# Where a causal convolution's running sums lie, which engine takes which taps, and where its group norms stand

## The chip, the core and the metric

The kernel runs on one core of one Trainium2 chip. Four engines compute: TensorE (PE in the rows; PEld is its weight load), VectorE (DVE), ScalarE (ACT) and GpSimd (POOL). SyncE (SP) issues most of the loads. SBUF is the large on-chip memory, PSUM the small one of eight banks into which TensorE writes; a bank holds 512 float32 values in each of 128 partitions. The metric is the device time of one execution in microseconds, the median over runs.

## What is computed

Two decoder layers for 256 tokens of width 1024, all in float32. The change touches the mixer of the first layer, whose two head groups share one input projection and one output projection:

```
u = h @ w_in                                   # 2560 columns
u_conv, u_sb = split(u, [1024])
val, gate = split(u_conv, 2)                   # 512 channels each
y = val * sigmoid(gate)
y = causal_depthwise_conv(y, conv_w) + conv_b  # 31 taps per channel
mean and variance of y over each 64 channels   # 8 groups
a_out = silu((y - mean) * rsqrt(var + 1e-5) * norm_g + norm_b)
b_out = stick_breaking_attention(q, k, v from u_sb)   # 8 heads of 64
mix = concat([a_out, b_out]) @ w_out
```

Behind it come a mixture of experts, the second layer's mixer, a second mixture of experts and a last norm.

## The kernel before

Activations lie transposed: channels in the partitions, the 256 tokens along the row. The 512 convolution channels are four tiles `yp[:, k]` of 128x286 (30 zeros ahead of the tokens), so tap `j` of tile `k` is the slice `yp[:, k, j:j + T]` times one weight per partition. There are 4 x 31 = 124 such taps.

**The projections** (class `Projections`, line 434 for transposed outputs, 429 for natural ones) run five times over 1024 input channels: gate, val, q, k, v. Each has eight steps; a step takes one granule of weights, 128x512, split into a high and a low part (`split`, lines 60 and 61: ScalarE copies the high part, VectorE subtracts), and twelve matmuls (six in the natural form) of TensorE. Granules are split two steps ahead. In the projections of q, k and v a callback `step` behind every step issues some taps through `conv(n, m)`: `n` from the generator `taps`, `m` from `other_taps`.

**The taps.** `taps` is VectorE's share, 59 of them: 16 of tile 2, 12 of tile 1 and all of tile 0, each a scalar_tensor_tensor (line 570) that reads the running sum and writes it back, in SBUF (`yc`). `other_taps` is the share of the other two engines, 65: all of tile 3, the last 15 of tile 2, 19 of tile 1 in a sum of its own (`more`); ScalarE multiplies into a small buffer (line 584, three buffers), GpSimd adds (line 585). At its end VectorE adds `more` to tile 1 (line 587).

**The heads.** Four passes `cc`, of two heads each. A pass has the sums over later keys on TensorE (`sums`, tile `zc`), VectorE's subtraction (`weights`, lines 666 and 667), ScalarE's exponential (line 668), the attention product (`attend`, line 680) and its split (`attended`, lines 685 and 686). Between these stand taps, `fill(n)` (steps of the conditioning matmuls, line 195, which need no result of the mixer) and, in the third pass, the first weights of the output product.

**The group norms.** `group_norm(h)` for two tiles at a time: a mean by a matmul with a block matrix (`gm`, line 691), VectorE's subtraction (692), ScalarE's square, a second matmul (`gv`, 697), reciprocal root on VectorE and ScalarE (699 to 701), VectorE's product (703). It is a generator; the code advances `gn[0]` (tiles 0 and 1) and `gn[1]` (tiles 2 and 3) by hand.

**The output product** (class `Output`, line 464) takes the heads' half first, in eight steps, then the convolution's half.

The order on every engine is the order of the code (a manual schedule). PSUM banks for short-lived tiles come from `bank`: two of the tag `ps`, one of the tag `pq`, in turn. Weights stream through a ring of 16 buffers of 1 MB; a load is issued when the buffer's last reader is done.

Of the kernel before, what the change touches and what calls it, by code (L numbers as in the profile page):

```python
# [15 lines left out]
T = 256  # L16
# [13 lines left out]
def trunk(ctx: ExitStack, tc: tile.TileContext, x, c, ada_w, ada_b, norm_mix, norm_ffn,  # L30
# [14 lines left out]
    turn = [0]  # L45

    def bank(name, two=False):
        tag, bufs = ("ps", 2) if two or turn[0] % 3 < 2 else ("pq", 1)
        turn[0] += not two
        return psum.tile([128, 512], F32, tag=tag, name=name, bufs=bufs)  # L50
# [459 lines left out]
    def even_mixer(pool, n01, late):  # L510
# [49 lines left out]

        def taps():

            sums = [[(2, j) for j in range(16)] + [(1, j) for j in range(12)], [(0, j) for j in range(31)]]
            while any(sums):
                sums.sort(key=len)
                k, j = sums[1].pop(0)
                if j == 0:
                    V.tensor_scalar(yc[:, k], yp[:, k, 0:T], epar[:, k, 0:1], epar[:, k, 31:32], op0=OP.mult, op1=OP.add)
                else:
                    V.scalar_tensor_tensor(yc[:, k], yp[:, k, j:j + T], epar[:, k, j:j + 1], yc[:, k],  # L570
                                           op0=OP.mult, op1=OP.add)
                yield

        def other_taps():
            more = pool.tile([128, T], F32, name="more")
            for k, js, y in ((3, range(31), yc[:, 3]), (2, range(16, 31), yc[:, 2]), (1, range(12, 31), more)):
                for j in js:
                    if k == 3 and j == 0:
                        G.tensor_scalar(y, yp[:, k, 0:T], epar[:, k, 0:1], epar[:, k, 31:32], op0=OP.mult, op1=OP.add)
                    elif k == 1 and j == 12:  # L580
# [5 lines left out]
                    yield  # L586
            V.tensor_tensor(yc[:, 1], yc[:, 1], more, op=OP.add)
# [13 lines left out]
        with tc.tile_pool(name="pj0", bufs=4, space=bass.MemoryType.PSUM) as banks:  # L601
# [10 lines left out]
            project(1, val)  # L612
            project(2, lambda h, b: S.activation(qT[:, 2 * h:2 * h + 2], b, AF.Copy, scale=0.125),
                    step=lambda k: conv(1 + k % 2, 1 + k % 2))
            project(3, lambda h, b: S.activation(kT[:, 2 * h:2 * h + 2], b, AF.Copy),
                    step=lambda k: conv(1 + k % 2, 1 + k % 2))
            vn = pool.tile([128, 2, 512], F32, tag="sv", name="vn")
            project(4, lambda t, b: S.activation(vn[:, t], b, AF.Copy), True, step=lambda k: conv(1 + k % 2, 1 + k % 2))
# [92 lines left out]
        conv(2, 4)  # L711
        minus(0)
        softplus(0)
        conv(2, 0)
# [3 lines left out]
        conv(2, 2)  # L718
        for cc in range(4):
# [26 lines left out]
        next(gn[1])  # L746
        next(steps)
        next(gn[1])
        next(gn[0])
# [940 lines left out]
```

## Time and profile before

| | |
|---|---|
| median of 3 runs | 781.63 us (779.17 to 783.79) |
| the profiled execution | 781.72 us, its span 780.0 us |
| TensorE busy | 720.2 us, 92% of the span |
| VectorE busy | 315.1 us, 40% |
| ScalarE busy | 235.0 us, 30% |
| GpSimd busy | 120.8 us, 15% |
| read from HBM | 280.59 MB, 361 GB/s over the span |

The shares are means over stages with different limits. The mixer of the first layer runs from about 33 to 180 us; its last three projections from 57.7 to 102 us, the heads from 104 to 145 us, the output product to about 180 us. The first experts start near 200 us.

### The profile page before, as it was taken

What the parts mean: (1) busy time and instruction counts of PE and PEld (TensorE: products, weight loads), DVE (VectorE), ACT (ScalarE), POOL (GpSimd) and SP (SyncE); (2) the same over time, 40 slices, a digit from 0 to 9 for tenths busy, and PEclk for the clock granted to TensorE, in tenths of its full rate; (3) what the DMA queues carried; (4) which work ended last, traced back from release to release, by engine and by line L of the source; (5) the groups of instructions that cost most, each with busy time, mean ns of one, the idle gap of its engine ahead of it and who ended that gap; (6) DMA issues with size and microseconds to landing.
All of it is one profiled execution on the core that took longest, in us unless ns stands there. A gap on an engine that the chain in (4) does not pass through costs nothing. (4 is left out here: it accounts for less than half of the span.)

```text
span 780.0 us, 10577 instructions
## 1 busy us (share of the span) xinstructions
PE 720.2 (92%) x4121; PEld 395.7 (51%) x4121; DVE 315.1 (40%) x567; ACT 235.0 (30%) x441; POOL 120.8 (15%) x168
## 2 busy tenths in 40 slices
PE   6898788898999999999888899999999999999995
PEld 4398643476434434443234577678534335444333
DVE  3459979475204113122114846454512214113214
ACT  3457667454102102111112535453401101001012
POOL 1357658022000000000003600010300000000000
PEclk9999999999999999999999999999899999999999
DMA  8999759953999999999999998497699999999994
GB/s 356 384 373 420 313 196 409 360 204 147 353 411 409 409 410 408 409 409 409 409 408 397 394 411 341 165 394 301 258 379 411 409 408 409 409 410 409 409 407 159
DMA packets 74712, 282.45 MB, mean 362 GB/s; under 512 B 5194, under 2 KB 6438, under 8 KB 69530
## 3 DMA queue, kind: packets, MB, share of 16 engines
q1 hardware_dynamic: 73122, 278.68, 91.1%
q0 software_dynamic: 1344, 2.64, 0.9%
q8 instruction: 34, 0.56, 0.3%
q10 hardware_dynamic: 184, 0.34, 0.1%
q14 instruction: 28, 0.23, 0.1%
HBM read 280.59 MB, written 1.05 MB: 361 GB/s over the span
## 5 line engine op out<-in xcount | busy, mean ns | idle before, releaser
L1272 PE MATMUL g<-w,xg 128*64 128x512 f32 x512 | 114.8, 597 | 1.9 <-DMA w<-in_moe_w_gate_dram 1.8
L1272 PE MATMUL u<-w,xg 128*64 128x512 f32 x496 | 111.3, 595 | 3.9 <-DMA w<-in_moe_w_up_dram 3.0
L1305 PE MATMUL dn<-w,at 128*64 128x512 f32 x448 | 100.2, 596 | 3.0 <-DMA w<-in_moe_w_down_dram 1.8
L1284 DVE TENSOR_TENSOR act<-sg,u 128x512 f32<-128x512 f32 (+1 forms) x18 | 11.1, 628 | 155.8 <-PE u L1272 155.8
L1272 PEld LDWEIGHTS u<-w,xg 128*64 128x64 f32 x496 | 34.7, 137 | 74.4 <-issue 62.7
L1272 PEld LDWEIGHTS g<-w,xg 128*64 128x64 f32 x512 | 35.0, 137 | 68.3 <-issue 60.5
L434 PE MATMUL pj<-hT,g 128*128 128x256 f32 x480 | 61.3, 285 | 6.1 <-DVE g L61 4.8
L61 DVE TENSOR_TENSOR g<-wi,g 128x512 fp32r<-128x512 f32 x72 | 57.0, 801 | 23.6 <-ACT g L60 23.4
L1305 PEld LDWEIGHTS dn<-w,at 128*64 128x64 f32 x448 | 31.4, 137 | 64.0 <-issue 55.4
L434 PEld LDWEIGHTS pj<-hT,g 128*128 128x128 f32 x480 | 57.7, 188 | 10.1 <-DVE g L61 6.9
L464 PE MATMUL po<-cat,g 128*128 128x256 f32 x372 | 52.9, 296 | 3.9 <-ACT gsr L1026 1.7
L60 ACT ACTIVATE g<-wi 128x512 fp32r<-128x512 f32 x72 | 44.4, 626 | 38.2 <-PE pj L434 20.7
L429 PE MATMUL pj<-g,hT 128*128 128x512 f32 x192 | 50.3, 412 | 6.0 <-ACT hT L355 3.1
L464 PEld LDWEIGHTS po<-cat,g 128*128 128x128 f32 x372 | 48.1, 201 | 9.3 <-issue 2.7
L195 PE MATMUL ada<-ad,cond 128*32 128x512 f32 x384 | 49.6, 626 | 3.0 <-DMA ad<-in_ada_w_dram 3.0
L429 PEld LDWEIGHTS pj<-g,hT 128*128 128x128 f32 x192 | 35.6, 193 | 20.1 <-DVE g L61 4.2
L570 DVE SCALAR_TENSOR_TENSOR yc<-yp,epar,yc 128x256 f32<-128x256 f32 x56 | 41.5, 756 | 2.2 <-POOL yc L585 1.7
L585 POOL TENSOR_TENSOR yc<-yc,cv 128x256 f32<-128x256 f32 x45 | 39.2, 872 | 19.7 <-ACT cv L584 12.0
L1295 DVE COPY at<-at 128x512 f32<-128x512 f32 x14 | 9.7, 692 | 67.3 <-PE at L1294 67.3
L1337 ACT ACTIVATE ys<-y 128x512 fp32r<-128x512 f32 x28 | 16.9, 625 | 64.2 <-DVE y L1327 59.3
L1280 ACT ACTIVATE sg<-g 128x512 f32<-128x512 f32 x14 | 8.4, 597 | 89.3 <-PE g L1272 89.3
L1331 ACT ACTIVATE y<-dn,cw 128x512 f32<-128x512 f32 x7 | 4.8, 687 | 100.5 <-PE dn L1305 100.5
(381 smaller groups left out, 869.8 us busy)
## 6 DMA issues: line engine op xcount, KB each, us to landing
w<-in_moe_w_gate_dram SPq DMA_DIRECT2D x64, 1024.0 KB, 15.5
w<-in_moe_w_up_dram SPq DMA_DIRECT2D x62, 1024.0 KB, 18.5
w<-in_moe_w_down_dram SPq DMA_DIRECT2D x61, 1024.0 KB, 18.1
ad<-in_ada_w_dram SPq DMA_DIRECT2D x48, 1024.0 KB, 9.0
wi<-in_w_in_even_dram SPq DMA_DIRECT2D x20, 512.0 KB, 12.2
wi<-in_w_in_odd_dram SPq DMA_DIRECT2D x14, 512.0 KB, 12.5
wo<-in_w_out_even_dram SPq DMA_DIRECT2D x4, 1024.0 KB
wo<-in_w_out_odd_dram SPq DMA_DIRECT2D x4, 1024.0 KB, 18.1
```

The costliest lines, as they stand in the source:

```text
L60: S.activation(g[0], w, AF.Copy)
L61: (eng or V).tensor_tensor(g[1], w, g[0].bitcast(F32), op=OP.subtract)
L195: PE.matmul(acc[32 * j:32 * j + 32, :], lhsT=cond[:, k, :], rhs=w[:, k - (i if n == 2 else 2 * i), c0:c0 + 512], start=i == 0, stop=i == 4 ...
L429: PE.matmul(bs[t], lhsT=self.h[j][:, k, t * 128:(t + 1) * 128], rhs=g[i], start=k == 0 and p == 0, stop=k == 7 and p == 2)
L434: PE.matmul(bs[c // 2][:, (c % 2) * T:(c % 2 + 1) * T], lhsT=g[i][:, c * 128:(c + 1) * 128], rhs=self.h[j][:, k, :], start=k == 0 and c % ...
L464: PE.matmul(self.acc[kd // 2][:, (kd % 2) * T:(kd % 2 + 1) * T], lhsT=block(g[wi], kd % 4), rhs=cats[ci][:, k, :], start=start and kd % 2 ...
L570: V.scalar_tensor_tensor(yc[:, k], yp[:, k, j:j + T], epar[:, k, j:j + 1], yc[:, k], op0=OP.mult, op1=OP.add)
L585: G.tensor_tensor(y, y, p, op=OP.add)
L1272: PE.matmul(b[64 * e:64 * e + 64, :], lhsT=xg[:, k, o + 64 * e:o + 64 * e + 64], rhs=we[:, e, k % 2 * 512:k % 2 * 512 + 512], start=k == 0 ...
L1284: V.tensor_tensor(a[:, n], sg[:, n], ub[:, n], op=OP.mult)
L1305: PE.matmul(bs[h][64 * e:64 * e + 64, :], lhsT=at[k][:, 64 * e:64 * e + 64], rhs=r[:, e], start=k == 0, stop=k == 3)
L1337: S.activation(ys[:, 0, n], y[h], AF.Copy)
```

## The change

VectorE's running sums move from SBUF to one PSUM bank, tag `pq` (`conv` in the rows). A bank has room for two tiles, so tiles 2 and 3 are summed side by side, 31 taps each, and then 12 taps of tile 1 in tile 2's room; the last tap of each writes to `yc`. VectorE has 74 taps now. ScalarE and GpSimd keep 50: all of tile 0 and 19 of tile 1. While the sums live, `bank` gives `ps` alone.

In the three projections `between(k)` issues 13 taps of VectorE per projection (39 in all, 36 before) and 6 of the others (18 in all, 36 before). The counts in the heads go up. When `other_taps` ends it first issues all that is left of `taps`. The group norms stand behind the last head, tiles 2 and 3 first.

```diff
     def bank(name, two=False):
+        two = two or kept[0]
         tag, bufs = ("ps", 2) if two or turn[0] % 3 < 2 else ("pq", 1)
...
+        SHARE = 12
         def taps():
-            sums = [[(2, j) for j in range(16)] + [(1, j) for j in range(12)], [(0, j) for j in range(31)]]
-            while any(sums):
-                sums.sort(key=len)
-                k, j = sums[1].pop(0)
+            bank_ = psum.tile([128, 512], F32, tag="pq", name="conv", bufs=1)
+            rooms = {k: bank_[:, i * T:(i + 1) * T] for i, k in ((0, 2), (1, 3), (0, 1))}
+            for k, j in [(k, j) for j in range(31) for k in (2, 3)] + [(1, j) for j in range(SHARE)]:
+                last = 30 if k > 1 else SHARE - 1
+                out_ = yc[:, k] if j == last else rooms[k]
...
-                    V.scalar_tensor_tensor(yc[:, k], yp[:, k, j:j + T], epar[:, k, j:j + 1], yc[:, k],
+                    V.scalar_tensor_tensor(out_, yp[:, k, j:j + T], epar[:, k, j:j + 1], rooms[k],
                                            op0=OP.mult, op1=OP.add)
                 yield
+            kept[0] = False
         def other_taps():
-            for k, js, y in ((3, range(31), yc[:, 3]), (2, range(16, 31), yc[:, 2]), (1, range(12, 31), more)):
+            for k, js, y in ((0, range(31), yc[:, 0]), (1, range(SHARE, 31), more)):
...
+            for _ in ds:
+                pass
             V.tensor_tensor(yc[:, 1], yc[:, 1], more, op=OP.add)
...
+        def between(k):
+            conv(1 + (k % 3 > 0), k % 4 > 0)
...
-                    step=lambda k: conv(1 + k % 2, 1 + k % 2))
+                    step=between)
...
-        conv(2, 4)
+        conv(3, 5)
         minus(0)
         softplus(0)
-        conv(2, 0)
+        conv(3, 1)
...
-        conv(2, 2)
+        conv(2, 4)
         for cc in range(4):
...
-            conv(2, 3)
+            conv(3, 3)
             fill((1, 1, 2, 2)[cc])
-            if cc == 3:
-                next(gn[0])
             attend(cc)
...
             conv(3, 2)
             if cc == 2:
-                next(gn[1])
                 next(steps)
                 next(steps)
+            if cc == 3:
+                next(gn[1])
             fill((2, 1, 2, 2)[cc])
         at.close()
         po.open(late())
         next(steps)
         next(gn[1])
+        conv(63, 63)
         next(steps)
+        next(gn[0])
         next(gn[1])
-        next(gn[0])
         next(steps)
...
+        next(gn[0])
         next(steps)
         next(gn[0])
         next(steps)
-        conv(63, 63)
```

On VectorE in the projection of q (`wi` weights, `g` their split, `yp` the padded input) this stands before:

```order
L570 SCALAR_TENSOR_TENSOR yc<-yp,epar,yc 128x256
L61 TENSOR_TENSOR g_700<-wi_636,g_700 128x512
L570 SCALAR_TENSOR_TENSOR yc<-yp,epar,yc 128x256 x2
L61 TENSOR_TENSOR g_726<-wi_723,g_726 128x512
L570 SCALAR_TENSOR_TENSOR yc<-yp,epar,yc 128x256
L61 TENSOR_TENSOR g_745<-wi_723,g_745 128x512
L570 SCALAR_TENSOR_TENSOR yc<-yp,epar,yc 128x256 x2
```

and this after:

```order
L62 TENSOR_TENSOR g_673<-wi_631,g_673 128x512
L574 SCALAR_TENSOR_TENSOR conv<-yp,epar,conv 128x256 x2
L62 TENSOR_TENSOR g_690<-wi_631,g_690 128x512
L574 SCALAR_TENSOR_TENSOR conv<-yp,epar,conv 128x256 x2
L62 TENSOR_TENSOR g_713<-wi_710,g_713 128x512
L574 SCALAR_TENSOR_TENSOR conv<-yp,epar,conv 128x256
L62 TENSOR_TENSOR g_732<-wi_710,g_732 128x512
L574 SCALAR_TENSOR_TENSOR conv<-yp,epar,conv 128x256 x2
```

The running sum is `conv`, in PSUM, and a step's taps are one or two in another rhythm.

On VectorE from the split of the third pass's output (`cat<-att`) to that of the fourth (`zs<-zs,zc` is the subtraction ahead of the last exponential), before:

```order
L686 TENSOR_TENSOR cat_1075<-att_1332,cat_1074 128x256
L570 SCALAR_TENSOR_TENSOR yc<-yp,epar,yc 128x256 x3
L692 TENSOR_TENSOR yc<-yc,gm_1348 128x512
L61 TENSOR_TENSOR g_1357<-wo_1353,g_1357 128x512
L61 TENSOR_TENSOR g_1360<-wo_1353,g_1360 128x512
L666 TENSOR_TENSOR zs_1271<-zs_1271,zc_1375 128x2x256
L667 TENSOR_TENSOR zs_1271<-zs_1271,zc_1375 128x2x128
L570 SCALAR_TENSOR_TENSOR yc<-yp,epar,yc 128x256 x2
L587 TENSOR_TENSOR yc<-yc,more 128x256
L692 TENSOR_TENSOR yc<-yc,gm_1404 128x512
```

and after:

```order
L697 TENSOR_TENSOR cat_1025<-att_1299,cat_1024 128x256
L572 TENSOR_SCALAR conv<-yp,epar 128x256
L574 SCALAR_TENSOR_TENSOR conv<-yp,epar,conv 128x256 x2
L62 TENSOR_TENSOR g_1319<-wo_1315,g_1319 128x512
L62 TENSOR_TENSOR g_1322<-wo_1315,g_1322 128x512
L574 SCALAR_TENSOR_TENSOR conv<-yp,epar,conv 128x256 x8
L574 SCALAR_TENSOR_TENSOR yc<-yp,epar,conv 128x256
L594 TENSOR_TENSOR yc<-yc,more 128x256
L677 TENSOR_TENSOR zs_1237<-zs_1237,zc_1337 128x2x256
L678 TENSOR_TENSOR zs_1237<-zs_1237,zc_1337 128x2x128
L697 TENSOR_TENSOR cat_1025<-att_1370,cat_1024 128x256
```

Before, two taps and the sum with `more` stand behind the last subtraction; now nine taps and that sum stand ahead of it, and the group norm's subtraction has gone from between.

On TensorE from the fourth pass's sums (`zc`) on (`ada` the conditioning matmuls, `gm` a group norm's mean, `gv` its variance, `po` the output product), before:

```order
L195 MATMUL ada_1319<-ad_1392,cond 32x512 x4
L195 MATMUL ada_1319<-ad_1398,cond 32x512 x4
L691 MATMUL gm_1404<-yc,bones 128x512
L680 MATMUL att_1409<-zs_1271,vn 64x256 x2
L680 MATMUL att_1409<-zs_1271,vn 64x128 x2
L195 MATMUL ada_1319<-ad_1416,cond 32x512 x4
L195 MATMUL ada_1319<-ad_1422,cond 32x512 x4
L697 MATMUL gv_1441<-gsq_1351,bones 128x512
L464 MATMUL po_1434<-cat_1074,g_1357 128x256
```

and after:

```order
L196 MATMUL ada_1286<-ad_1358,cond 32x512 x4
L196 MATMUL ada_1286<-ad_1364,cond 32x512 x4
L691 MATMUL att_1370<-zs_1237,vn 64x256 x2
L691 MATMUL att_1370<-zs_1237,vn 64x128 x2
L702 MATMUL gm_1377<-yc,bones 128x512
L196 MATMUL ada_1286<-ad_1382,cond 32x512 x4
L196 MATMUL ada_1286<-ad_1388,cond 32x512 x4
L708 MATMUL gv_1407<-gsq_1380,bones 128x512
L465 MATMUL po_1400<-cat_1024,g_1319 128x256
```

The means have moved behind the last `att`, one at once, the other (not in these rows) behind a step of output products.

## Rows read from the trace of the kernel before

**Rows 1.** The page, part 2: the DMA engines' busy tenths in 40 slices.

```profile
DMA  8999759953999999999999998497699999999994
```

**Rows 2.** TensorE's waits from 57 to 102 us: total, times, longest.

```profile
PE pj L434 <- DVE g L61: 4.6, 9, 1.2
```

**Rows 3.** Busy time by stage: stretch, length, then each engine; clock, DMA share, GB/s.

```profile
58.70:102.00 43.30, 36.67 (x235) 30.92 (x233) 41.90 (x56) 27.75 (x59) 28.14 (x33) 1.00 0.84 336
102.00:135.50 33.50, 27.50 (x191) 13.22 (x191) 29.80 (x41) 26.93 (x51) 26.20 (x30) 0.95 0.83 334
...
145.20:165.10 19.90, 17.75 (x132) 14.59 (x130) 12.80 (x22) 14.84 (x25) 2.69 (x2) 1.00 0.68 251
165.10:200.00 34.90, 31.24 (x222) 25.18 (x222) 19.33 (x49) 10.62 (x21) 7.03 (x6) 0.85 0.58 220
```

**Rows 4.** Timeline of VectorE in the projections: start, length, instruction, count, idle before.

```profile
58.73 0.68 DVE L61 TENSOR_TENSOR g<-wi,g 128x512 fp32r<-128x512 f32 x1
...
79.45 1.21 DVE L61 TENSOR_TENSOR g<-wi,g 128x512 fp32r<-128x512 f32 x1
80.59 0.95 DVE L570 SCALAR_TENSOR_TENSOR yc<-yp,epar,yc 128x256 f32<-128x256 f32 x1
...
97.42 0.99 DVE L570 SCALAR_TENSOR_TENSOR yc<-yp,epar,yc 128x256 f32<-128x256 f32 x2
98.33 0.69 DVE L61 TENSOR_TENSOR g<-wi,g 128x512 fp32r<-128x512 f32 x1
98.94 0.48 DVE L570 SCALAR_TENSOR_TENSOR yc<-yp,epar,yc 128x256 f32<-128x256 f32 x1
99.33 0.69 DVE L61 TENSOR_TENSOR g<-wi,g 128x512 fp32r<-128x512 f32 x1
```

**Rows 5.** Timeline of ScalarE in the projection of val, which has no taps.

```profile
52.49 0.63 ACT L60 ACTIVATE g<-wi 128x512 fp32r<-128x512 f32 x1 [0.78 <-PE pj L434]
53.89 0.63 ACT L60 ACTIVATE g<-wi 128x512 fp32r<-128x512 f32 x1 [0.77 <-PE pj L434]
```

**Rows 6.** Timeline of TensorE from the last projection to the output product.

```profile
96.56 5.40 PE L429 MATMUL pj<-g,hT 128*128 128x512 f32 x22 [1.22 <-DVE g L61]
104.05 1.12 PE L631 MATMUL z<-qT,kT 64*128 64x256 f32 x4 [2.09 <-ACT vn L618]
...
111.84 0.70 PE L659 MATMUL zc<-ze,later 128*128 128x256 f32 x2 [0.21 <-DVE ze L652]
...
131.76 0.87 PE L680 MATMUL att<-zs,vn 128*64 128x256 f32 x8 [2.02 <-ACT zs L668]
132.56 1.12 PE L691 MATMUL gm<-yc,bones 128*128 128x512 f32 x2
...
135.47 0.70 PE L659 MATMUL zc<-ze,later 128*128 128x256 f32 x2
...
141.72 2.02 PE L691 MATMUL gm<-yc,bones 128*128 128x512 f32 x2 [2.40 <-DVE yc L587]
143.67 1.55 PE L680 MATMUL att<-zs,vn 128*64 128x256 f32 x8
...
165.07 3.76 PE L464 MATMUL po<-cat,g 128*128 128x256 f32 x15 [1.36 <-DVE cat L769]
```

**Rows 7.** Timeline of GpSimd: a tap alone, the last taps, a split in layer two.

```profile
89.37 0.74 POOL L585 TENSOR_TENSOR yc<-yc,cv 128x256 f32<-128x256 f32 x1 [2.14 <-ACT cv L584]
...
138.90 1.66 POOL L585 TENSOR_TENSOR more<-more,cv 128x256 f32<-128x256 f32 x2 [2.25 <-ACT cv L584]
...
524.56 1.30 POOL L61 TENSOR_TENSOR g<-wo,g 128x512 fp32r<-128x512 f32 x1 [11.18 <-ACT g L60]
```

**Rows 8.** Timeline of VectorE: instructions that read PSUM.

```profile
129.82 0.68 DVE L666 TENSOR_TENSOR zs<-zs,zc 128x512 f32<-128x512 f32 x1
...
139.68 0.41 DVE L667 TENSOR_TENSOR zs<-zs,zc 128x256 f32<-128x256 f32 x1
...
524.88 0.48 DVE L1063 SCALAR_TENSOR_TENSOR cat<-ot,opar,cat 128x256 fp32r<-128x256 f32 x1 [2.27 <-ACT cat L1062]
```

More of the change, by code (lines that the diff above doesn't have):

```diff
@@ L42, in trunk @@
     ctx.enter_context(tc.manual_schedule())
-    turn = [0]
+    turn, kept = [0], [False]
     def bank(name, two=False):
+        two = two or kept[0]
         tag, bufs = ("ps", 2) if two or turn[0] % 3 < 2 else ("pq", 1)
@@ L558, in val @@
             V.tensor_tensor(yp[:, 2 * h:2 * h + 2, 30:30 + T], b, sg[:, 2 * h:2 * h + 2], op=OP.mult)
+        SHARE = 12
         def taps():
-            sums = [[(2, j) for j in range(16)] + [(1, j) for j in range(12)], [(0, j) for j in range(31)]]
-            while any(sums):
-                sums.sort(key=len)
-                k, j = sums[1].pop(0)
+            bank_ = psum.tile([128, 512], F32, tag="pq", name="conv", bufs=1)
[3 more added lines that the diff above has]
+                out_ = yc[:, k] if j == last else rooms[k]
                 if j == 0:
-                    V.tensor_scalar(yc[:, k], yp[:, k, 0:T], epar[:, k, 0:1], epar[:, k, 31:32], op0=OP.mult, op1=OP.add)
+                    V.tensor_scalar(out_, yp[:, k, 0:T], epar[:, k, 0:1], epar[:, k, 31:32], op0=OP.mult, op1=OP.add)
                 else:
-                    V.scalar_tensor_tensor(yc[:, k], yp[:, k, j:j + T], epar[:, k, j:j + 1], yc[:, k],
+                    V.scalar_tensor_tensor(out_, yp[:, k, j:j + T], epar[:, k, j:j + 1], rooms[k],
                                            op0=OP.mult, op1=OP.add)
                 yield
+            kept[0] = False
         def other_taps():
             more = pool.tile([128, T], F32, name="more")
-            for k, js, y in ((3, range(31), yc[:, 3]), (2, range(16, 31), yc[:, 2]), (1, range(12, 31), more)):
+            for k, js, y in ((0, range(31), yc[:, 0]), (1, range(SHARE, 31), more)):
                 for j in js:
-                    if k == 3 and j == 0:
+                    if k == 0 and j == 0:
                         G.tensor_scalar(y, yp[:, k, 0:T], epar[:, k, 0:1], epar[:, k, 31:32], op0=OP.mult, op1=OP.add)
-                    elif k == 1 and j == 12:
+                    elif k == 1 and j == SHARE:
                         S.activation(y, yp[:, k, j:j + T], AF.Copy, scale=epar[:, k, j:j + 1])
@@ L612, in even_mixer @@
             project(1, val)
+            kept[0] = True
             project(2, lambda h, b: S.activation(qT[:, 2 * h:2 * h + 2], b, AF.Copy, scale=0.125),
-                    step=lambda k: conv(1 + k % 2, 1 + k % 2))
+                    step=between)
             project(3, lambda h, b: S.activation(kT[:, 2 * h:2 * h + 2], b, AF.Copy),
-                    step=lambda k: conv(1 + k % 2, 1 + k % 2))
+                    step=between)
             vn = pool.tile([128, 2, 512], F32, tag="sv", name="vn")
-            project(4, lambda t, b: S.activation(vn[:, t], b, AF.Copy), True, step=lambda k: conv(1 + k % 2, 1 + k % 2))
+            project(4, lambda t, b: S.activation(vn[:, t], b, AF.Copy), True, step=between)
         at = ExitStack()
```

## The prediction

> **What bounds the kernel now.** I read the slices first, then the wait list, then busy time by stage, then the timelines. [rows 1] is the DMA engines' share in 40 slices of 19.5 us: full in most, but 7 and 5 around 78 to 117 us and 5 and 3 around 156 to 195 us. There the even mixer sets the pace and the weight stream waits for it; from 200 us on the stream runs without a gap for 160 us. So a microsecond saved ahead of 165 us is a microsecond less idle DMA, and it should reach the end. The wait list for TensorE in the three last projections names one releaser, VectorE's part of the weight split [rows 2]. The busy times agree: from 58.7 to 102 us VectorE is busy 41.90 of 43.30 us, while TensorE is busy 36.67, ScalarE 27.75 and GpSimd 28.14 [rows 3]. **VectorE bounds the projections.**
>
> Why it is so loaded is in its timeline [rows 4]. The same split takes 1.21 us at 79.45 and 0.69 us at 98.33; the same tap 0.95 us at 80.59 and 0.48 us at 98.94. The long ones lie in stretches where GpSimd adds taps, the short ones in gaps of GpSimd. So an instruction of VectorE with two SBUF tensors pays about 0.5 us when it meets an add of GpSimd. Spacing, alone: a split 0.61 us (98.33 to 98.94), a tap 0.39 us (98.94 to 99.33), two taps of which the second waits for the first 0.91 us (97.42 to 98.33), so 0.52 and 0.39.
>
> **What a tap in PSUM costs.** After the change a tap reads one SBUF tensor (yp) and a PSUM bank. Two rows show such instructions beside a busy GpSimd. At 524.88 a scalar_tensor_tensor of 128x256 with a PSUM tensor, a pointer scalar and an SBUF tensor takes 0.48 us while GpSimd works from 524.56 to 525.86; at 139.68 a subtraction with one PSUM operand takes 0.41 us inside two adds of GpSimd [rows 7, 8]. Neither is stretched, so I take 0.39 us for a tap and 0.52 us for one that waits on its neighbour. All taps now write one bank, and the built order holds each until the last one has finished, so the second of a pair always pays 0.52. What no row shows is an instruction that writes PSUM, or reads and writes one bank. Bounds: 0.39 us as above; from the other side the second half of a 512-wide row: 0.68 us at 129.82 against 0.41 us at 139.68 [rows 8], so 0.27 us for 256 elements more, which a bank that is passed twice would cost. I take the near end, since the read side behaves so.
>
> [...]
>
> **Projections (58.73 to 101.96).** From the first split at 58.73 to the end of the last at 100.02 VectorE does 22 splits with the taps of 22 steps: 41.3 us. After: step k issues one tap where k is a multiple of 3, else two; in 22 steps that is 8 single taps and 14 pairs. 22 x 0.61 + 8 x 0.39 + 14 x 0.91 = 13.4 + 3.1 + 12.7 = 29.3 us. GpSimd's adds fall from 36 to 18, of which 17 lie here, 0.74 us each when alone [rows 7]: it is busy some 12.6 of 32 us. The splits still have two SBUF tensors. A split starts inside an add with a chance of 0.39 and then waits half of one: 0.39 x 0.37 = 0.14 us, 22 times 3.2 us. So VectorE needs 32.5 us. Bounds: no meeting, 29.3; each add meets a split, 17 x 0.53 = 9.0 more, 38.3. TensorE has a floor: in projection 1, which has no taps, ScalarE's casts follow TensorE every 1.40 us [rows 5], so 24 steps from 57.7 (one us ahead of VectorE's first split) end at 91.3 at best. With 32.5 us the last split ends at 91.2, and TensorE 1.9 us behind it as now (101.96 against 100.02 [rows 4, 6]): 93.1. **8.8 us saved**, between 3.0 (38.3 us of VectorE) and 10.6 (TensorE's floor).
>
> ScalarE loses 15 tap products and GpSimd 15 adds in all; both have room [rows 3]. The weight loads are issued far ahead and no wait of TensorE here is on DMA [rows 2].
>
> **First heads.** The logits wait 2.09 us after the projections for the copy of v, which stands in ScalarE's queue behind products that wait for GpSimd, which waited for VectorE's sums of the same channels [rows 6]. Now GpSimd's channels are its own, and that coupling is gone; the copy itself stays: 1.1 us saved. From the first zc at 111.84 to the fourth at 135.47 are 23.63 us. The group mean in it (132.56, 1.12 us) moves out. The wait of 2.02 us ahead of 131.76 is ScalarE's exponential, which waited for VectorE's subtraction behind three stretched taps; three at up to 0.95 us [rows 4], some 2.4 with their overlap, shrink to some 1.4: 1.0. The small waits of the heads ahead give perhaps 0.3. **2.4 saved.** I cost ScalarE's seven products per head at nothing: they stand there now too.
>
> **Last head: a new queue.** In the fourth pass the helper drains the remaining taps at once: nine in a row in one channel, then the sum with `more`, all ahead of the subtraction that the last attention waits for. Now that stretch takes 9.75 us (135.47 to 145.22), 2.40 us of it a wait for the group mean, 2.02 us the mean itself [rows 6]. After: VectorE still has three taps and two splits to do when the fourth zc starts, so the nine begin some 1.5 us after it; 8 x 0.52 + 0.39 = 4.6, the sum 0.5, then from the subtraction to the attention 1.94 us (129.82 to 131.76): it starts at 8.5 and lasts 0.87 to 1.55. That is 9.4 to 10.1 against 9.75: **nothing saved**, the two means' time is eaten by the nine taps. TensorE sits some 4 us there.
>
> **Output products.** Both group means now stand behind the last head: 1.12 us at the rate of 132.56, 2.02 us at that of 141.72, so 2.2 to 3.1 us of TensorE in a stretch that is busy 17.75 of 19.90 [rows 3, 6]. VectorE's subtraction, ScalarE's square and the chain after it come later too, each behind a step of output products. Some of it fills idle time: **1.5 us lost**, between 0.7 and 3.1.
>
> The narrower choice of banks (two instead of three while the sums live) I cost at nothing: the heads' outputs and the columns of the modulation are read out within a microsecond or two and follow each other by some 7 us.
>
> **Sum.** 8.8 + 1.1 + 2.4 + 0 - 1.5 = 10.8 us. The profiled execution took 781.7 us (its span 780.0), the median is 781.6: 781.7 - 10.8 = **770.9 us**. Behind 165 us nothing changes; the stretch from 165.1 to 200 has a DMA share of 0.58 [rows 3], so the stream has idle time to give up and the gain passes on.
>
> **Rivals.**
> - TensorE is the floor in the projections and the waits of the heads vanish: 1.8 + 2.0 + 0.8 more, 766.3 us. For it: ScalarE's casts are paced by TensorE, so adds may fall beside the taps and not the splits. Chance 0.17.
> - GpSimd's adds meet nearly every split, as they do today. Then 3.0 and not 8.8: 776.7 us. Against it: half the adds are gone. Chance 0.15.
> - A PSUM bank that is read and written at once costs a second pass, 0.27 us per tap. Projections: 36 x 0.27 = 9.7 more, so 0.9 lost instead of 8.8 saved; the heads, with six taps each on a VectorE that has about 0.8 us to spare, lose 2.5 of their gain; the nine taps 2.4. Sum: -3.8, **785.5 us, slower**. It turns from about 0.2 us per tap. For it: no row shows such an instruction; against it: the read side is free. Chance 0.09.
> - The gain is made and given back behind 200 us because the stream, not the mixer, set the start of the experts: 780 us. Against it the idle share above. Chance 0.04.
>
> The forecast itself has 0.55. About 0.5% (3.9 us) is what a measurement can tell from no change. Faster: 0.55 + 0.17 + two thirds of 0.15 and a little = 0.83; the same: the rest of the second rival and the last, 0.08; slower 0.09. The range: 765.5 (first rival with a little less idling in the output products) to 777.7, which leaves out the slower case, the last, and the worst of the meetings.
>
> **What would show it.** Taps of some 0.48 us in the projections whatever GpSimd does, splits between 0.7 and 0.9 us in the mean; the three projections in 35 to 36 us instead of 44; VectorE no longer the releaser of most waits of TensorE there. Behind the fourth zc an idle TensorE of about 4 us, ended by the exponential of the last head, with nine taps ahead of it on VectorE. I am wrong if the taps take 0.7 us or more, if splits stay at 1.2 us, or if the time between the start of the output products' second half and the experts changes.

## The result and the profile after

The changed kernel takes **773.75 us** (median of 4 runs, 772.73 to 774.67), the kernel before beside it 780.5 us: a ratio of **0.9904 (0.9881 to 0.9927; here and below, in brackets, a 95% interval)**. By the medians 6.8 us are saved where 10.8 were forecast. The profiled execution of after has a span of 773.0 us, before's has 780.0. The direction was right and the time lies in the range, but the sum was too good, and its terms missed in both directions: part of the nearness is luck.

Busy time by stage in after, cut at the same events as in [rows 3] (stretch, length, then PE, PEld, DVE, ACT, POOL, each with its count; clock, DMA share, GB/s):

```profile
59.40:92.80 33.40, 33.40 (x235) 30.86 (x234) 32.09 (x61) 21.61 (x43) 15.95 (x18) 1.00 1.02 416
92.80:123.60 30.80, 24.82 (x190) 12.00 (x189) 24.23 (x43) 26.75 (x51) 23.73 (x28) 1.00 0.91 350
123.60:135.50 11.90, 5.30 (x37) 2.60 (x33) 9.02 (x17) 2.79 (x5) 3.70 (x5) 0.81 1.00 384
135.50:159.00 23.50, 20.50 (x136) 15.45 (x134) 14.22 (x24) 16.10 (x27) 2.69 (x2) 0.95 0.54 200
```

The first row is the projections of q, k and v: TensorE is busy all the time, 33.40 of 33.40 us, and VectorE has 32.09 us of work instead of 41.90. The third row is the new trouble: behind the fourth pass's sums TensorE is busy 5.30 of 11.90 us.

The timeline of TensorE in after (start, length, instruction, count, idle before and what ended it), as [rows 6]:

```profile
81.43 11.38 PE L430 MATMUL pj<-g,hT 128*128 128x512 f32 x48
93.49 0.70 PE L642 MATMUL z<-qT,kT 64*128 64x256 f32 x4 [0.69 <-ACT vn L629]
...
100.83 0.70 PE L670 MATMUL zc<-ze,later 128*128 128x256 f32 x2 [1.34 <-DVE ze L663]
...
106.58 0.87 PE L691 MATMUL att<-zs,vn 128*64 128x256 f32 x8 [1.59 <-ACT zs L679]
...
123.56 0.70 PE L670 MATMUL zc<-ze,later 128*128 128x256 f32 x2
...
134.00 1.55 PE L691 MATMUL att<-zs,vn 128*64 128x256 f32 x8 [6.59 <-ACT zs L679]
135.48 2.08 PE L702 MATMUL gm<-yc,bones 128*128 128x512 f32 x2
...
145.92 1.12 PE L708 MATMUL gv<-gsq,bones 128*128 128x512 f32 x2 [1.61 <-ACT gsq L705]
...
159.00 2.42 PE L465 MATMUL po<-cat,g 128*128 128x256 f32 x15 [1.37 <-DVE cat L780]
```

From such starts the spans can be set against each other, piece by piece. The column of the prediction is its saving for that piece.

| piece | before | after | saved | predicted |
|---|---|---|---|---|
| to the first product with the gate (VectorE, `yp`) | 57.41 | 58.13 | -0.7 | 0 |
| to the end of the projections (101.96; 92.81) | 44.6 | 34.7 | 9.9 | 8.8 |
| to the first `zc` (111.84; 100.83) | 9.9 | 8.0 | 1.9 | 1.1 |
| to the fourth `zc` (135.47; 123.56) | 23.6 | 22.7 | 0.9 | 2.4 |
| to the end of the last `att` (145.22; 135.55) | 9.8 | 12.0 | -2.2 | 0 |
| to the second half of the output product (165.07; 159.00) | 19.9 | 23.5 | -3.6 | -1.5 |
| to the end (780.0; 773.0) | 614.9 | 614.0 | 0.9 | 0 |

The first row lies ahead of all changed instructions; the two executions differ there by themselves. At 159.00 after is 6.1 us ahead, at the end 7.0: what is saved in the mixer reaches the end, as the idle DMA of [rows 1] promised. Of the 11.9 us by which after is ahead at the fourth `zc`, 5.8 are lost behind it: 2.2 up to the last `att`, 3.6 in the output product.

### The profile page after: what moved, and what is told of

It reads as the page before. It is cut to its first block, busy times and chain, and to the rows that moved or that the text cites. A ratio compares the mean times of both kernels' runs of the same rounds, so it can differ in the third digit from the quotient of the medians.

```text
span 773.0 us, 10543 instructions
## 1 busy us (share of the span) xinstructions
PE 712.5 (92%) x4121; PEld 391.7 (51%) x4121; DVE 304.5 (39%) x582; ACT 228.7 (30%) x426; POOL 107.5 (14%) x153
## 5 line engine op out<-in xcount | busy, mean ns | idle before, releaser
L1283 PEld LDWEIGHTS u<-w,xg 128*64 128x64 f32 x496 | 34.7, 137 | 74.2 <-issue 62.1
L1283 PEld LDWEIGHTS g<-w,xg 128*64 128x64 f32 x512 | 34.9, 137 | 69.4 <-issue 60.6
L62 DVE TENSOR_TENSOR g<-wi,g 128x512 fp32r<-128x512 f32 x72 | 52.4, 736 | 24.4 <-ACT g L61 24.1
L435 PE MATMUL pj<-hT,g 128*128 128x256 f32 x480 | 59.1, 283 | 1.4 <-DVE hT L335 1.2
L574 DVE SCALAR_TENSOR_TENSOR conv<-yp,epar,conv 128x256 f32<-128x256 f32 x68 | 33.0, 485 | 1.4
L1338 DVE SCALAR_TENSOR_TENSOR y<-dn,cw,g2fn 128x512 f32<-128x512 f32 x14 | 10.5, 747 | 54.1 <-PE dn L1316 47.9
```

The costliest lines, as they stand in the source:

```text
L62: (eng or V).tensor_tensor(g[1], w, g[0].bitcast(F32), op=OP.subtract)
L435: PE.matmul(bs[c // 2][:, (c % 2) * T:(c % 2 + 1) * T], lhsT=g[i][:, c * 128:(c + 1) * 128], rhs=self.h[j][:, k, :], start=k == 0 and c % ...
L574: V.scalar_tensor_tensor(out_, yp[:, k, j:j + T], epar[:, k, j:j + 1], rooms[k], op0=OP.mult, op1=OP.add)
L1283: PE.matmul(b[64 * e:64 * e + 64, :], lhsT=xg[:, k, o + 64 * e:o + 64 * e + 64], rhs=we[:, e, k % 2 * 512:k % 2 * 512 + 512], start=k == 0 ...
L1338: V.scalar_tensor_tensor(y, bs[h], cw, g2row[:, parts[h]], op0=OP.mult, op1=OP.mult)
```

## What the taps cost in PSUM

VectorE in the projections of after, and GpSimd's adds beside it (timelines):

```profile
82.78 0.69 DVE L62 TENSOR_TENSOR g<-wi,g 128x512 fp32r<-128x512 f32 x1
83.39 0.48 DVE L574 SCALAR_TENSOR_TENSOR conv<-yp,epar,conv 128x256 f32<-128x256 f32 x1
...
84.38 1.01 DVE L574 SCALAR_TENSOR_TENSOR conv<-yp,epar,conv 128x256 f32<-128x256 f32 x2
85.29 1.14 DVE L62 TENSOR_TENSOR g<-wi,g 128x512 fp32r<-128x512 f32 x1
```

```profile
83.80 3.22 POOL L590 TENSOR_TENSOR yc<-yc,cv 128x256 f32<-128x256 f32 x3 [2.63 <-ACT cv L589]
```

GpSimd adds from 83.80 to 87.02. In that time two taps take 1.01 us, as in its gaps (1.00 us at 81.64); the split behind them takes 1.14 us where the one in the gap takes 0.69. A tap that reads and writes one PSUM bank is not stretched by GpSimd here, the split with its two SBUF tensors still is. A single tap, at 80.50 inside GpSimd's add of 79.95 to 81.17, takes 0.48 us; with its sum in SBUF it took 0.95 at 80.59 in before [rows 4], inside adds of 80.50 to 82.14.

Two experiments part the place of the sums from the rest of the change. The first differs from after in that place alone.

**The whole change without PSUM (e2).** The sums go back to SBUF, all else stays.

```diff
-            bank_ = psum.tile([128, 512], F32, tag="pq", name="conv", bufs=1)
-            rooms = {k: bank_[:, i * T:(i + 1) * T] for i, k in ((0, 2), (1, 3), (0, 1))}
+            rooms = {k: yc[:, k] for k in (2, 3, 1)}
```

> The changed kernel with VectorE's sums back in SBUF, all else as it is (shares, order, norms, two banks while the sums live). Theory of the port: a tap then has two SBUF tensors again and waits wherever GpSimd is adding, which is nearly half the time: taps of 0.65 to 0.75 us in the mean against 0.485, the three projections 37 to 40 us against 34.4, the kernel 777 to 780 us. Rival: the smaller share of GpSimd and ScalarE made the projections quick, not the place of the sums: taps near 0.5 us, 773 to 775 us.

Measured: 780.64 us, 1.0001 (0.9982 to 1.0020) of before. On the whole, all that the change moves besides is worth nothing without the bank. But not because the projections stay slow, as their busy times show (columns as in the stages of after):

```profile
59.40:94.60 35.20, 33.78 (x224) 29.11 (x222) 35.20 (x58) 21.25 (x42) 16.67 (x17) 1.00 0.98 398
```

VectorE is full, 35.20 of 35.20 us, and yet from the first product with the gate to their end the projections take 37.8 us (94.60 less 56.82), 44.6 before and 34.7 in after: there half of the rival holds, the smaller share by itself takes 6.8 us off. It is lost again behind them: from the first to the fourth `zc` it is 25.1 us (23.6 before), to the end of the last `att` 11.5 (9.8), to the second half of the output product 23.9 (19.9).

**PSUM alone (e3, and e10 once more).** The kernel before with its own shares, counts and norm places; only the sums of VectorE's 59 taps move to a bank (tiles 2 and 0 side by side, tile 1 behind tile 2), and `bank` leaves that one out.

```diff
+        two = two or kept[0]
...
+            bank_ = psum.tile([128, 512], F32, tag="pq", name="conv", bufs=1)
+            rooms = {k: bank_[:, i * T:(i + 1) * T] for i, k in ((0, 2), (1, 0), (0, 1))}
...
-                    V.scalar_tensor_tensor(yc[:, k], yp[:, k, j:j + T], epar[:, k, j:j + 1], yc[:, k],
+                    V.scalar_tensor_tensor(yc[:, k] if j == ends[k] else rooms[k], yp[:, k, j:j + T], epar[:, k, j:j + 1], rooms[k],
```

> The kernel before with one part of the change: VectorE's sums lie in a PSUM bank (tiles 0 and 2, then 1, with tile 2's sixteen taps first), while shares, counts per step and the group norms stay as before. Theory of the port: taps of 0.48 us, the three projections near TensorE's floor, 34 to 36 us against 44.3, the kernel 771 to 774 us; the splits, which meet twice as many adds of GpSimd as in the changed kernel, stay at 0.9 to 1.1 us. Rival (the shares do it): projections 41 us or more, 777 to 780 us.

Measured: 768.05 us, **0.9827 (0.9796 to 0.9857)**, less than the theory's own 771 to 774. Beside later runs of the kernel before it was measured once more:

> Experiment e3 once more, unchanged, so that it, e8 and e9 stand beside the same runs of the kernel before. Theory: 0.983 of the kernel before, about 767 to 769 us, above e8 by some 2 us if e8's theory holds. Rival: within 1 us of e8, so that the moves of taps among the engines bring nothing beyond the place of the sums.

Measured: 768.76 us, 0.9848 (0.9804 to 0.9891), and 769.16 us for e8 (below) beside it. The rival holds. By the two ratios PSUM alone is 4 to 6 us better than the whole change, though the second interval just reaches that of the change. VectorE's costliest groups from 55 to 200 us (count, busy us, mean ns, idle us before and what ended it), one fence each for before, after, the whole change in SBUF, and PSUM alone:

```profile
L570 DVE SCALAR_TENSOR_TENSOR yc<-yp,epar,yc 128x256 f32<-128x256 f32 x56 | 41.5, 756 | 2.2 <-POOL yc L585 1.7
L61 DVE TENSOR_TENSOR g<-wi,g 128x512 fp32r<-128x512 f32 x24 | 23.1, 965 | 1.4 <-ACT g L60 1.4
```

```profile
L574 DVE SCALAR_TENSOR_TENSOR conv<-yp,epar,conv 128x256 f32<-128x256 f32 x68 | 33.0, 485 | 1.4
L62 DVE TENSOR_TENSOR g<-wi,g 128x512 fp32r<-128x512 f32 x24 | 18.5, 769 | 2.2 <-ACT g L61 2.1
```

```profile
L573 DVE SCALAR_TENSOR_TENSOR yc<-yp,epar,yc 128x256 f32<-128x256 f32 x71 | 46.0, 682 | 0.4
L62 DVE TENSOR_TENSOR g<-wi,g 128x512 fp32r<-128x512 f32 x23 | 17.8, 774 | 0.7 <-ACT g L61 0.7
```

```profile
L574 DVE SCALAR_TENSOR_TENSOR conv<-yp,epar,conv 128x256 f32<-128x256 f32 x53 | 25.6, 483 | 0.9
L62 DVE TENSOR_TENSOR g<-wi,g 128x512 fp32r<-128x512 f32 x24 | 22.4, 932 | 1.4 <-ACT g L61 1.4
```

The tap's price hangs on where its sum lies, 756 and 682 ns in SBUF, 485 and 483 ns in PSUM; the split's on how much GpSimd adds, 965 and 932 ns with 36 adds planned in the projections, 769 and 774 ns with 18. PSUM alone keeps the 36 adds and pays for them in its splits, and yet loses little by it, as its busy times in the projections show:

```profile
59.40:93.00 33.60, 33.48 (x228) 29.61 (x226) 33.17 (x55) 28.18 (x58) 31.09 (x34) 1.00 1.01 415
```

TensorE is full here too, 33.48 of 33.60 us, VectorE nearly, and GpSimd works 31.09 us of it. From the first product with the gate to their end the projections take 35.7 us (93.00 less 57.29), 34.7 in after: once TensorE sets the pace, taking half of the adds from GpSimd buys one microsecond more. For it, 12 of the 15 taps that VectorE has taken over stand in the heads (35 there, 74 less 39, instead of 23, 59 less 36), with 32 products of the other engines instead of 29, ten instead of six of them ahead of the first pass.

Where the 4 to 6 us lie shows against PSUM alone with the norms placed as in the change (e9 below). The whole change is 1.4 us shorter up to the first `zc` (42.7 against 44.1 us from the first product with the gate), 1.0 us longer from there to the fourth, 5.8 us longer to the end of the last `att`, and 1.1 us longer to the second half of the output product.

## Where the gain went: the drained taps

VectorE in after from the end of its third-pass work to the last subtraction, and ScalarE's exponential (timelines):

```profile
124.82 2.21 DVE L62 TENSOR_TENSOR g<-wo,g 128x512 fp32r<-128x512 f32 x2
126.95 4.15 DVE L574 SCALAR_TENSOR_TENSOR conv<-yp,epar,conv 128x256 f32<-128x256 f32 x8
131.13 0.48 DVE L574 SCALAR_TENSOR_TENSOR yc<-yp,epar,conv 128x256 f32<-128x256 f32 x1
131.72 0.42 DVE L594 TENSOR_TENSOR yc<-yc,more 128x256 f32<-128x256 f32 x1
132.06 0.68 DVE L677 TENSOR_TENSOR zs<-zs,zc 128x512 f32<-128x512 f32 x1
```

```profile
133.11 0.84 ACT L679 ACTIVATE zs<-zs 128x768 f32<-128x768 f32 x1 [7.40 <-DVE zs L678]
```

The nine taps and the sum with `more` take from 126.95 to 132.06; the subtraction stands behind them, ScalarE idles 7.40 us and TensorE 6.59 us.

**The taps behind the last head (e1).** The drain goes; what is left of the taps is issued where the code asks for it later, most of it behind the last attention product; the counter keeps the sum with `more` for the last of these places.

```diff
-            for _ in ds:
-                pass
+            yield
             V.tensor_tensor(yc[:, 1], yc[:, 1], more, op=OP.add)
...
+        did = [0]
         def conv(n, m):
...
             for i in range(m):
-                next(os_, None)
+                if did[0] < 50 or n > 9:
+                    did[0] += 1
+                    next(os_, None)
```

> The changed kernel, but the taps that are left when the other engines have done theirs are not drained ahead of the last head's subtraction: six go behind that subtraction, the last three and the sum with more behind the first step of output products. Theory: the nine taps in a row (4.7 us on VectorE, after 2.2 us of stretched splits) hold the last exponential; it then starts some 5 us earlier (7.4 us of idle ScalarE ahead of it fall to about 2.5), and the kernel takes 768 to 770 us against 773.75. Rival: the chain of the group norms behind it (matmul, subtraction, square, matmul, root) sets when the convolution's half of the output product can start, and the 5 us are waited for there: 772 to 774 us.

Measured: **769.5 us**, 0.9849 (0.9820 to 0.9877), as the theory has it. TensorE's timeline:

```profile
122.68 0.70 PE L673 MATMUL zc<-ze,later 128*128 128x256 f32 x2
...
128.02 0.87 PE L694 MATMUL att<-zs,vn 128*64 128x256 f32 x8 [1.50 <-ACT zs L682]
...
136.92 1.85 PE L705 MATMUL gm<-yc,bones 128*128 128x512 f32 x2 [1.82 <-DVE yc L593]
...
153.82 2.54 PE L465 MATMUL po<-cat,g 128*128 128x256 f32 x9 [1.37 <-DVE cat L783]
```

From the fourth `zc` to the last `att` it is 5.3 us instead of 10.4. The taps are not free behind it: the second mean waits 1.82 us for their sum. In all the drain costs 0.0055 of before's time, 4.3 us, which is most of what the whole change lies behind PSUM alone.

**The first mean early again (e4).** In the changed kernel only the mean of tiles 2 and 3 goes back into the third pass.

```diff
             if cc == 2:
+                next(gn[1])
                 next(steps)
                 next(steps)
-            if cc == 3:
-                next(gn[1])
```

> The changed kernel with the first group norm's mean (tiles 2 and 3, whose sums are done by then) at the end of the third pass, as the kernel before had it; the other norm stays behind the last head. Theory: its 2.1 us of matmul and the subtraction and square behind it go into the 6.6 us in which TensorE waits for the last head, and the 23.5 us from the last head to the convolution's half of the output product become 21 to 22: 771 to 772.5 us. Rival: only the second norm's chain (its second matmul waits 1.6 us) sets that time: 773 to 774.5 us.

Measured: 776.05 us, 0.9935 (0.9907 to 0.9962). That is above both forecasts, with an interval that overlaps the change's: no gain is shown. Counted from the first `zc` (100.00, 100.83 in after), the mean costs 1.5 us ahead of the fourth (24.2 us instead of 22.7), the last `att`, still behind the nine taps, comes 0.9 us later (34.1 instead of 33.2), and the second half of the output product starts when it did, after 58.2 us in both. The wait ahead of the second `gv` is still 1.60 us.

**Both together (e5).** The taps behind the last head and the first mean early.

> e1_taps_behind_last_head and e4_first_norm_early in one: the left-over taps behind the last head's subtraction, and the first norm's mean at the end of the third pass. Alone the first gained 4 us and the second nothing, because the third pass's end is followed by a wait for the last head anyway. Theory: with the queue ahead of the last head gone, the first mean's subtraction and square are done before the first step of output products and the second mean's is what remains; a gain of 0 to 1.5 us over e1: 768 to 769.5 us. Rival: the mean now stands on the path to the fourth zc (1.1 us of TensorE plus VectorE's subtraction between taps and splits) and costs what it saves or more: 769.5 to 771 us.

Measured: 770.25 us, 0.9873 (0.9852 to 0.9894), no better than the late taps alone, as the rival has it. The mean of the other pair now waits 2.13 us, for the sum with `more`.

**The second mean one step later (e8).** On top of the kernel with products in the projections (next section), where that wait of 2.13 us stands too.

```diff
         next(steps)
-        next(gn[0])
         next(gn[1])
         next(steps)
+        next(gn[0])
...
+        next(steps)
         next(gn[0])
         next(steps)
         next(gn[0])
-        next(steps)
```

> Kernel e6 (products in the projections, late taps, first norm early) with the second norm's mean one step of output products later, and its second matmul and product one step later too, without any change to what is computed. In e6 TensorE waited 2.13 us for the sum with `more` ahead of that mean. Theory (the wait is idle time that a step of products can fill, since the sum is ready some 2 us after TensorE arrives): the mean no longer waits, the convolution's half of the output product starts 1.5 to 2 us sooner (near 148.5 instead of 150.3), and the time falls to 765 to 766 us where the kernel before takes 780. Rival (the chain behind the mean, subtraction, square, second matmul, root, product and silu, then ends last): the wait moves to that half's own start, and the time is e6's, 767 to 768.

Measured: 769.16 us, 0.9843 (0.9802 to 0.9883), the ratio that this kernel had without the edit. The mean's wait fell to 0.68 us, but 0.44 us came ahead of `gv` and 0.66 us among the output products just ahead of the second half, which began 50.9 us behind the first `zc`, 51.0 without the edit. The rival holds: the chain behind the mean ends last, and the idle time moves along it.

**Norms behind the last head, PSUM alone (e9).** The places of the norms as in the change, in the kernel that has only the sums in PSUM.

```diff
             fill((1, 1, 2, 2)[cc])
-            if cc == 3:
-                next(gn[0])
             attend(cc)
...
             if cc == 2:
-                next(gn[1])
                 next(steps)
                 next(steps)
+            if cc == 3:
+                next(gn[1])
...
         next(steps)
+        next(gn[0])
         next(gn[1])
-        next(gn[0])
         next(steps)
...
+        next(gn[0])
         next(steps)
         next(gn[0])
```

> The kernel before with its sums in PSUM and its shares unchanged (experiment e3, 0.9827 of before), with one part of the change added: the two group norms behind the last head, placed as in the changed kernel. Theory (the placing of the norms costs, whatever the shares): the fourth pass is some 2 us shorter without the mean's wait of 1.77 us and the mean itself, but the output products' first half grows by 3 to 4 us, so the time is e3's plus 1 to 2.5 us: 769 to 770.5, ratio near 0.985. Rival (the placing is free or a gain, and the cost of the whole change lies in the shares and the drained taps alone): 766 to 768, ratio 0.983 or less.

Measured: 769.04 us, 0.9852 (0.9808 to 0.9896), beside 768.76 us and 0.9848 without the edit. The number lies in the theory's range, which was set against the 0.9827 of the first run; beside the second run the placing is free. Its timeline shows why: the last `att` comes 5.33 us behind the fourth `zc` (123.08, 128.41) instead of 6.64 (124.43, 131.07 in the second run of PSUM alone), and a new wait of 1.59 us ahead of the second `gv` takes it back; the second half starts at 151.64 against 151.81.

## Where the gain went: the products in the heads

TensorE's waits for ScalarE between the first and the fourth `zc`, those not yet shown, before and after (`acol` are the columns of the modulation):

```profile
116.25 0.87 PE L680 MATMUL att<-zs,vn 128*64 128x256 f32 x8 [0.25 <-ACT zs L668]
...
123.74 0.87 PE L680 MATMUL att<-zs,vn 128*64 128x256 f32 x8 [0.66 <-ACT zs L668]
125.41 0.75 PE L204 MATMUL acol<-ident,arow 128*128 128x128 f32 x4 [0.80 <-ACT arow L200]
```

```profile
115.32 0.74 PE L205 MATMUL acol<-ident,arow 128*128 128x128 f32 x4 [1.12 <-ACT arow L201]
...
120.90 0.87 PE L691 MATMUL att<-zs,vn 128*64 128x256 f32 x8 [1.26 <-ACT zs L679]
```

**More products in the projections (e6).** On top of both edits together: one product in every step of the projections, 24 instead of 18, and fewer ahead of the first head.

```diff
         def between(k):
-            conv(1 + (k % 3 > 0), k % 4 > 0)
+            conv(1 + (k % 3 > 0), 1)
...
-        conv(3, 5)
+        conv(3, 2)
         minus(0)
...
-        conv(2, 4)
+        conv(2, 1)
         for cc in range(4):
```

> e5 with six more of the other engines' taps in the projections (one in every step, 24 instead of 18) and six fewer ahead of the first heads (2, 1 and 1 products instead of 5, 1 and 4). Theory: ScalarE's products hold the first heads (the first attention waits 1.59 us for the exponential, which stands behind four products); the first zc comes 0.5 to 1 us earlier and that wait falls below 0.5 us, the projections stay at TensorE's floor (34.4 us): 1.5 to 2.5 us less than e5. Rival: the six adds meet VectorE's splits in the projections and give back what the heads gain: no difference to e5.

Measured: **767.35 us**, 0.9843 (0.9825 to 0.9861), beside 770.25 for its parent: 2.9 us. TensorE in this kernel:

```profile
99.37 0.70 PE L673 MATMUL zc<-ze,later 128*128 128x256 f32 x2
...
104.15 0.87 PE L694 MATMUL att<-zs,vn 128*64 128x256 f32 x8 [0.61 <-ACT zs L682]
```

The first `zc` no longer waits (1.34 us in after) and the first `att` waits 0.61 instead of 1.59 us. From the first product with the gate to their end the projections take 35.0 us, 34.7 in the parent; from that end to the fourth `zc` it is 29.9 us instead of 32.2. So the six products cost 0.4 us where TensorE is the bound and save 2.3 us where ScalarE is. The rest of the 2.9 lies behind the fourth `zc`, where the edit changes nothing: there TensorE's work behind equal waits took longer in the parent (last section), whose profiled execution has a mean granted clock of 0.977 against 0.987.

**Light heads (e7).** The other way to relieve them, on top of both edits again: the projections get back the counts of the kernel before, ahead of the first pass stand two products instead of ten, and the passes have four each instead of seven.

```diff
-            conv(1 + (k % 3 > 0), k % 4 > 0)
+            conv(1 + k % 2, 1 + k % 2)
...
-        conv(3, 5)
+        conv(3, 1)
...
-        conv(3, 1)
+        conv(3, 0)
...
-        conv(2, 4)
+        conv(2, 1)
...
-            conv(0, 2)
+            conv(0, 1)
             weights(cc)
...
-            conv(3, 3)
+            conv(3, 2)
...
-            conv(3, 2)
+            conv(3, 1)
```

> e5 with the projections' taps as in the kernel before (36 and 36) and so 14 instead of 32 of the other engines' taps in the heads, 38 of VectorE's. Theory: with taps in PSUM the projections still run at TensorE's floor (34.3 us as in e3), and the heads, which ScalarE's seven products per pass hold, shorten from 22.7 us between first and fourth zc to TensorE's own 20.5 to 21.5: 3 to 4 us less than e5, near 765 us. Rival: the heads are held by the chain through VectorE, ScalarE and TensorE, not by the products: 22 us or more, the kernel within 1 us of e5.

Measured: 771.88 us, 0.9883 (0.9847 to 0.9919), which can't be told from its parent's 0.9873 and is far from 765. Half of the theory holds:

```profile
104.54 0.87 PE L694 MATMUL att<-zs,vn 128*64 128x256 f32 x8
...
113.04 0.60 PE L673 MATMUL zc<-ze,later 128*128 128x256 f32 x2
...
120.87 2.04 PE L705 MATMUL gm<-yc,bones 128*128 128x512 f32 x2 [2.34 <-DVE yc L574]
...
126.42 0.79 PE L673 MATMUL zc<-ze,later 128*128 128x256 f32 x2
```

The waits of the first two `att` are gone, and from the first `zc` (100.44) to the third (113.04) it takes 12.6 us, 15.1 in after (100.83 to 115.90). One microsecond of that is due to the products ahead of the first pass (14.1 us in the kernel of e6, with four there and seven in every pass), 1.5 to those in the passes. But VectorE has done 36 taps in the projections, not 39, so tiles 2 and 3 are whole later: the mean that stands in the third pass waits 2.34 us, and the one behind the last head 3.70. The gain of the passes is lost there.

## Why the prediction was right, and where its terms were off

- **The bound, right.** VectorE was the limit of the projections. After the change the trace shows no wait of TensorE on anything from 57 to 93 us (before, 4.6 us on VectorE in line 434 [rows 2] and 2.0 more in line 429, three times).
- **The price of a tap, right.** 0.48 us and a pitch of 0.52 for a dependent pair, GpSimd busy (0.48 us at 80.50, a pair 1.01 at 84.38) or not (0.48 at 87.86, a pair 1.00 at 81.64). The in-place bank, which no row showed, has no second pass: the slower rival fell (0.27 us per tap; 485 ns is the mean of 68). Nor does a single tap cost more in PSUM: 0.48 us is what one from SBUF alone took at 98.94 [rows 4].
- **The projections, 9.9 instead of 8.8.** The step that failed is what sets the end: I took VectorE's 32.5 us as the limit, just above TensorE's floor. VectorE did need 32.09 us, but TensorE, full, set the end, at 92.81 where 93.1 was forecast. Since this execution came to the projections 0.7 us later, the term reads 9.9. The first half of the first rival, TensorE as the floor, is what happened.
- **The first heads, 1.9 instead of 1.1.** The wait for the copy of v fell from 2.09 to 0.69 us, 1.4 saved (with the old shares, in PSUM alone, it is 1.47 us). TensorE's work behind it went from 7.58 us (104.05 to 111.84 less 0.21 idle) to 6.00 (93.49 to 100.83 less 1.34): that is the clock, 0.78 and 1.00 in these two stretches (last section), the first four `z` matmuls took 0.70 us instead of 1.12 [rows 6], and the prediction had no term for it. A new wait of 1.34 us for VectorE's `ze`, 0.21 before, took 1.1 of it back.
- **The heads, 0.9 instead of 2.4.** The step that failed is the price of ScalarE's products: "seven products per head at nothing: they stand there now too". Seven per pass they are still, but ten instead of six stand ahead of the first pass, and the prediction did not count these. So the waits did not shrink by 1.3 us: between the first and the fourth `zc` TensorE's waits were 3.73 us before (0.25, 0.66, 0.80, 2.02) and are 3.97 now (1.59, 1.12, 1.26). What is saved is the mean's 1.12 us. PSUM alone with the norms behind, six products ahead, has no wait at the first `att` and takes 21.7 us, 1.9 saved. Nor are the seven themselves free: the light heads put three fewer at 1.5 us in two passes.
- **The last head, -2.2 instead of 0.** The drain was costed rightly, 4.6 us for the nine taps and 1.94 us from the subtraction to the attention (132.06 to 134.00). What was mis-sized is when the nine begin: 3.4 us behind the fourth `zc`, not 1.5, since the three taps had hardly begun then, and the two splits behind them met adds of GpSimd and took 2.21 us, 1.3 alone [rows 4]. And a cost that was seen was set against the means' gain and called nothing; the late taps show that it was 4.3 us to be had.
- **The output products, -3.6 instead of -1.5.** The two means took 2.08 and 1.02 us, the upper bound of the term. "Some of it fills idle time" failed: TensorE is busy 2.75 us more there (20.50 against 17.75) and idle 0.85 us more, as the second `gv` waits 1.61 us for the square. PSUM alone with its norms behind shows that by itself the placing is even: what the output products lose, the heads gain. Here the drained taps had eaten that gain.
- **Behind 165 us, right.** The mixer's gain arrives at the end; in [rows 1] the stream is full for 14 slices from 195 us, 273 us, where the prediction read 160. One sign of being wrong did show: from the second half of the output product to the experts' first matmul it is 33.5 us (159.00 to 192.53), 34.9 before (165.07 to 200.00). But that is a gain, and TensorE's clock: the fifteen matmuls at its start take 2.42 us, at 1.00 (159.0 to 163.0 us), instead of 3.76 [rows 6], at 0.57 (165.1 to 169.0 us). The rival of a gain lost downstream fell, and so did the one of adds that meet every split (769 ns in the mean, not 1.2 us).
- **The first rival's other half, wrong.** Its 766.3 us needed the waits of the heads to vanish with TensorE at its floor. PSUM alone and the kernel with products in the projections come to within 2.5 us of it; the change itself put nine taps and more products in the way.
- **The total, in part luck.** Two terms were too low, by 1.1 and 0.8 us, and three too high, by 1.5, 2.2 and 2.1. The prediction costed the bank only together with the new shares; that the bank alone would do better was not among its rivals.

What stays open: whether one order has both the short projections of the change and the short heads of PSUM alone. The best kernels can't be told apart by these runs: PSUM alone with 0.9827 and 0.9848, the one with products in the projections with 0.9843, and the change with late taps with 0.9849. So that the drain costs is shown; that the new shares cost the whole kernel anything besides is not, though the heads are 1.0 us longer with them.

## What to carry to other kernels

When VectorE accumulates beside a busy GpSimd, try its running sum in PSUM before any sharing out anew: here the place alone gave 12 to 13.5 us of 781 (1 less 0.9848 and 0.9827), and the rest of the change took back 4 to 6. Two remedies for one bound don't add up: the bank alone took 8.8 us off the projections, the smaller share alone 6.8, both together 9.9. Once another engine is the bound of a stage, work moved out of it for the old bound's sake gains little there, and can cost more in the next. Of a queue that is drained at once, ask which instruction stands behind it: nine short taps ahead of one subtraction made two engines idle for 7 us.

## What the runs showed of the hardware

- **Behind some waits of TensorE its granted clock is lower, so that such a wait is paid twice.** Behind the wait of 2.09 us ahead of the logits of before the granted clock is 0.57 from 104 to 108 us (0.50 from 106 to 107), and the four `z` matmuls take 1.12 us; in after, behind 0.69 us, they take 0.70 us at 1.00 (92.8 to 97.0 us). Behind the wait of 6.59 us it is 0.50 from 134.0 to 137.5 us: eight `att` matmuls take 1.55 us instead of 0.87 (at 120.90), two `gm` 2.08 instead of 1.02 (at 141.85). It is not so behind every wait. In the projections of before, with waits of up to 1.2 us, the clock is 1.00 [rows 2, 3], and behind equal waits the work took longer or not, as the same mean shows in two kernels, with both edits (e5) and with products in the projections (e6); the twelve output products behind it take 3.30 and 2.01 us, and the mean granted clock of the two executions is 0.977 and 0.987:

```profile
136.97 1.79 PE L705 MATMUL gm<-yc,bones 128*128 128x512 f32 x2 [2.13 <-DVE yc L593]
...
134.74 1.10 PE L705 MATMUL gm<-yc,bones 128*128 128x512 f32 x2 [2.13 <-DVE yc L593]
```

So too behind the 1.37 us ahead of the second half of the output product: fifteen matmuls take 2.42 us in after, at 1.00, and 3.82 with the first mean early, close to the 3.76 of before, behind 1.36 us, at 0.57. What decides it the runs don't show; a microsecond or two between two profiled executions can be this alone.

- **A tap in PSUM stays at its price even beside a GpSimd that never stops.** In PSUM alone GpSimd adds without a gap in the trace, and VectorE's pairs of taps take 1.00 us while the split beside them takes 1.14 (timelines of GpSimd and VectorE):

```profile
77.45 17.87 POOL L590 TENSOR_TENSOR yc<-yc,cv 128x256 f32<-128x256 f32 x18
```

```profile
78.98 1.00 DVE L574 SCALAR_TENSOR_TENSOR conv<-yp,epar,conv 128x256 f32<-128x256 f32 x2
79.89 1.14 DVE L62 TENSOR_TENSOR g<-wi,g 128x512 fp32r<-128x512 f32 x1
```

- **Two sums in one bank follow each other as if they were one.** The pair of taps belongs to different tiles, and in SBUF, in a gap of GpSimd, it takes 0.87 us (the whole change in SBUF, at 82.68: VectorE's timeline below); in the bank 1.01. It hangs on the writing: the last taps of tiles 2 and 3 in after, which read the bank and write to SBUF, take 0.87 us (at 121.15). Whether the chip orders the two or the waits built into the program do, no run parts.

```profile
82.68 0.87 DVE L573 SCALAR_TENSOR_TENSOR yc<-yp,epar,yc 128x256 f32<-128x256 f32 x2
```
